# The last blocks of a hybrid decoder trunk: a kept order on VectorE and ACT, the products with the final weights on GpSimd, a last half block in two pieces

## The chip, the cores and the metric

The kernel runs on one core of one Trainium2 chip. The time is device microseconds for one execution, and the median of the runs is taken. "The profiled execution" is one further run, recorded by the hardware profiler. TensorE is called PE in the profile, VectorE DVE, ScalarE ACT, GpSimd POOL and SyncE SP.

## What is computed

A decoder trunk of two layers on 512 tokens of width 1024. Layer 0 is a convolution module and a feed-forward part, layer 1 is windowed attention and a feed-forward part. All that the change touches is the end: the down projection of the last feed-forward part, its residual, and the final RMSNorm.

```python
def rmsnorm(x, g):
    return x * lax.rsqrt(jnp.mean(x * x, axis=-1, keepdims=True) + EPS) * g
...
def swiglu_ffn(x, w_up, w_down):
    gate, up = jnp.split(x @ w_up, 2, axis=-1)
    return (jax.nn.silu(gate) * up) @ w_down
...
        h = h + swiglu_ffn(rmsnorm(h, norm_ffn[l]), ffn_w_up[l], ffn_w_down[l])
    return rmsnorm(h, norm_final)
```

## The kernel before

**Numbers.** A matrix product runs as three passes: weights and activations are both split into a high and a low part (`split`, `split_weights`, L277 and L280), and high x high, high x low and low x high are added up in one PSUM bank. A bank holds 128 partitions x 512 columns of float32. There are eight.

**Most of the span** is this stream of products: weights come in chunks of 128x1024 by DMA (SP issues them, L244), ACT and VectorE split them ahead of use, TensorE multiplies. In layer 1 the feed-forward part runs over pairs of hidden tiles; for most pairs a seven-product scheme for 2x2 blocks is used, and its down projection (`low_pairs`, matmuls at L862) adds into the rows of h directly: VectorE at L871, GpSimd at L869.

**The end** (L1521 to L1549) is what the change rewrites. Here the tokens lie on the partitions, so that the sum over the 1024 channels is a sum along a row. The last pair of hidden tiles (`hid`, its high and low part) is multiplied with the last two rows of `w_down` chunks (`whole`, one for each half g of the 1024 columns). The loop runs over NBLK = 4 blocks b of 128 tokens, and in it over the two halves g of 512 columns:

- six matmuls (L1531) into one bank: 2 tiles of hidden rows x 3 passes, 512 columns each;
- VectorE, L1533: `v = bank * rs + h`, the finished rows of h for this block and half, into `room[:, g]` in SBUF;
- ACT, L1535: the square of v with the sum of the row into a column of `ss` (the page shows it as an ACTIVATE and an ACTIVATION_READ_ACCUMULATOR);
- VectorE, L1537 for g = 0 and L1539 for g = 1: two small instructions on 128x1 that make the mean of squares plus EPS from the two sums;
- GpSimd, L1541, once a block: that number to the power -0.5 (called `last`, in the profile `rs<-ss,mhalf`);
- VectorE, L1542: the product of v with the final norm's weights, `gain`, into `room[:, 2 + g]`;
- after both halves, the scaling by `last`: VectorE for g = 1 (L1546), ACT for g = 0 (L1548);
- two stores of 128x512 to the output (L1549), g = 1 by SP's queue and g = 0 by ACT's.

Each engine works through its own queue in order. The order within a queue is set when the program is built: a list scheduler takes the instructions by a model of time. `tc.issue_after(x)` holds an instruction behind x in the program's order; before the change, nothing of the kind is used in this end. What came out for VectorE is, from the first L1533 on (b.g of each): L1533 0.0, L871, L1542 0.0, L1537 of block 0, L871, L1533 1.0, L1542 1.0, L1533 0.1, L1542 0.1, L1533 1.1, L1539 of block 0, L1533 2.0, L1537 of block 1, L1542 1.1, L1546 of block 0, L1542 2.0, L1539 of block 1, L1533 2.1, L1537 of block 2, L1533 3.0, L1546 of block 1, L1542 2.1, L1533 3.1, L1542 3.0, L1539 of block 2, L1537 of block 3, L1542 3.1, L1539 of block 3, L1546 of blocks 2 and 3. TensorE finishes the banks in the order 0.0, 1.0, 0.1, 1.1, 2.0, 2.1, 3.0, 3.1. GpSimd has nothing in this end but the four powers.

Of the kernel before, what the change touches and what calls it, by code (L numbers as in the profile page):

```python
# [11 lines left out]
F32 = mybir.dt.float32  # L12
F32R = mybir.dt.float32r
AF = mybir.ActivationFunctionType
ALU = mybir.AluOpType
# [3 lines left out]
P = 128  # L19
D = 1024  # L20
# [8 lines left out]
NBLK = S // P  # L29
BAND = 2 * P  # L30
NBUCKET = 32
EPS = 1e-6
# [160 lines left out]
def hybrid_trunk(ctx: ExitStack, tc: tile.TileContext, xT, W, prm_in, wdw_in, sinks, relb, onehot, fin, lead, out):  # L193
    nc = tc.nc
# [4 lines left out]
    small = ctx.enter_context(tc.tile_pool(name="small", bufs=4))  # L199
# [5 lines left out]
    def uid(s):  # L205
        ctr[0] += 1
        return f"{s}{ctr[0]}"

    def bank():
        return ps.tile([P, 512], F32, tag="bank", name=uid("bank"))  # L210
# [4 lines left out]
    def temp():  # L215
        return tmp.tile([P, 512], F32, tag="tmp", name=uid("tmp"))
# [65 lines left out]
    def advance():  # L282
        u = stream["use"]
        share[1] += share[0]
        while share[1] >= 1:
            share[1] -= 1
            next(preparing[0], None)
        load(u + DMA_AHEAD)
        while stream["split"] < min(len(PLAN), u + SPLIT_AHEAD):
            i = stream["split"]  # L290
            stream["split"] += 1
            if i in NATIVE:
                splits[i] = (raws.pop(i), None)
                continue
            hi = wpool.tile([P, 1024], F32R, tag="whi", name=uid("whi"))
            lo = wpool.tile([P, 1024], F32R, tag="wlo", name=uid("wlo"))
            splits[i] = (hi, lo)
            split_weights(hi, lo, raws.pop(i))
# [21 lines left out]
    def pace():  # L320
        g = seen[0] = seen[0] + 1
        for j in list(jobs):
            while j[2] < due_at(j[1], g):
                j[2] += 1
                if next(j[0], "end") == "end":
                    jobs.remove(j)
                    break

    def tick(n):
        while n > 0 and background:  # L330
            if next(background[0], "end") == "end":
                background.pop(0)
            else:
                n -= 1
# [10 lines left out]
    def get(*key):  # L345
        advance()
        pace()
        due[0] += rate[0]
        tick(int(due[0]))
        due[0] -= int(due[0])  # L350
        i = stream["use"]
        assert PLAN[i] == key, (PLAN[i], key)
        stream["use"] += 1
        hi, lo = splits.pop(i)
        n = {"kv": 4, "up": 4, "q": 4}.get(key[0], 2)
        sh = dict(a=n)
        return tuple(w and w.rearrange("p (a b) -> p a b", **sh) for w in (hi, lo))
# [95 lines left out]
    mhalf = cpool.tile([P, 4], F32, tag="mhalf", name="mhalf")  # L453
# [295 lines left out]
    def new_gates(pool):  # L749
        return pool.tile([P, 2, 2, 2, 256], F32, tag="up", name=uid("up"), bufs=3)  # L750

    def plain_pair(pair, rows, pool):

        banks = accs(512)
        steps = None
        for half in range(2):
            for which in range(2):
                w = get("up", 1, pair, half, which)
                order = [(k, m) for k in range(4) for m in range(2)]
                if half == 1:  # L760
                    order = [(k, m) for m in range(2) for k in range(4)]
                for k, m in order:
                    mm3(banks[which * 2 + m], [a[:, k, m * P:(m + 1) * P] for a in w], rows.x[half * 4 + k],
                        half == 0 and k == 0, half == 1 and k == 3)
                if half == 0 and which == 0:
                    rows.rms.step1()
                    continue

                if pair == 0:
                    steps = steps or rows.sums()  # L770
                    for _ in range(1 + half):
                        next(steps, None)
        rs_bc = rows.rms.step2().rearrange("p (s q) -> p s q", s=2)
        c = new_gates(pool)
        for m in range(2):
            t = temp()
            nc.vector.tensor_mul(t.rearrange("p (s q) -> p s q", s=2), banks[m].rearrange("p (s q) -> p s q", s=2), rs_bc)
            nc.scalar.activation(t, t, AF.Silu)
            nc.vector.tensor_mul(c[:, m, :, 0, :], banks[2 + m].rearrange("p (s q) -> p s q", s=2),
                                 t.rearrange("p (s q) -> p s q", s=2))  # L780
        return c
# [62 lines left out]
    def rows_of(g, t):  # L844
        return hT[:, g * 4:(g + 1) * 4, t * P:(t + 1) * P]
# [427 lines left out]
    for pair in range(lo0, hi0):  # L1273
        c = seven_pair("up0", pair, rows0, z0.tile([P, 2, 2, 2, 256], F32, tag="z0", name=uid("up"), bufs=5))
# [8 lines left out]
    if True:  # L1283
# [6 lines left out]
        x, rms = nxt.x, nxt.rms  # L1290
# [8 lines left out]
        for half in range(2):  # L1299
            whi, wlo = get("kv", 0, half)  # L1300
# [7 lines left out]
        for half in range(2):  # L1308
            whi, wlo = get("kv", 1, half)
            for k in range(4):  # L1310
                xh, xl = xkv[half * 4 + k]
# [4 lines left out]
            if half == 0:  # L1316
                rs_bc = rms.step2()
                rs = rms.rs
# [4 lines left out]
        for n in range(4):  # L1323
            nc.vector.tensor_scalar(vq[:, n].rearrange("p a g c -> p (a g c)"), vb[n][:, 0:256], rs[:, n:n + 1], None,
                                    op0=ALU.mult)
# [126 lines left out]
        for part in range(2):  # L1452
            for g in range(2):
# [3 lines left out]
                if part == 0:  # L1457
# [3 lines left out]
                    for m0, kp in ((0, 0), (0, 1), (2, 0), (2, 1)) if g else ((0, 0), (2, 0), (0, 1), (2, 1)):  # L1461
                        order = [(k, m) for k in range(2) for m in (m0, m0 + 1)]
                        if kp:
                            order = [(k, m) for m in (m0, m0 + 1) for k in range(2)]
# [12 lines left out]
                for m in range(4):  # L1477
                    i = g * 4 + m
# [20 lines left out]
    for kind, pair in STEPS1:  # L1499
# [6 lines left out]
        if by_seven(1, pair):  # L1506
            c = seven_pair("up", pair, nxt, new_gates(pool7), flip if pair == SEVENS[0] else None)
        else:
            c = plain_pair(pair, nxt, pool7)
# [8 lines left out]
        gain = quads.tile([P, 2, D], F32, tag="quad", name=uid("gain"))[:, 0]  # L1518
        nc.sync.dma_start(gain, fin.to_broadcast([P, D]))

    whole = [get("down", 1, LAST, g) for g in range(2)]  # L1521
    for b in range(NBLK):
        tok, rs = slice(b * P, (b + 1) * P), nxt.rms.rs[:, b:b + 1]
        room = quads.tile([P, 4, 512], F32, tag="quad", name=uid("room"))
        ss = small.tile([P, 4], F32, tag="ss", name=uid("ss"))
        for g, (whi, wlo) in enumerate(whole):
            acc = bank()
            for k in range(2):
                xh, xl = (hid[:, e, k, tok] for e in range(2))
                for n, (x, w) in enumerate(((xh, whi), (xh, wlo), (xl, whi))):  # L1530
                    nc.tensor.matmul(acc, x, w[:, k, :], start=k == 0 and n == 0, stop=k == 1 and n == 2)  # L1531
            v, o = room[:, g], room[:, 2 + g]
            nc.vector.scalar_tensor_tensor(v.rearrange("p (i c) -> p i c", i=4), acc.rearrange("p (i c) -> p i c", i=4), rs,  # L1533
                                           rows_of(g, b), op0=ALU.mult, op1=ALU.add)
            nc.scalar.activation(temp(), v, AF.Square, accum_out=ss[:, g:g + 1])  # L1535
            if g == 0:
                nc.vector.tensor_scalar(ss[:, 2:3], ss[:, 0:1], 1.0 / D, EPS, op0=ALU.mult, op1=ALU.add)  # L1537
            else:
                nc.vector.scalar_tensor_tensor(ss[:, 3:4], ss[:, 1:2], 1.0 / D, ss[:, 2:3], op0=ALU.mult, op1=ALU.add)  # L1539
                last = small.tile([P, 1], F32, tag="rs1", name=uid("rs1"))  # L1540
                nc.gpsimd.tensor_tensor(last, ss[:, 3:4], mhalf[:, 0:1], op=ALU.pow)  # L1541
            nc.vector.tensor_mul(o, v, gain[:, g * 512:(g + 1) * 512])  # L1542
        for g in range(2):
            o = room[:, 2 + g]
            if g:
                nc.vector.tensor_scalar(o, o, last[:, 0:1], None, op0=ALU.mult)  # L1546
            else:
                nc.scalar.mul(o, o, last[:, 0:1])  # L1548
            (nc.sync if g else nc.scalar).dma_start(out[tok, g * 512:(g + 1) * 512], o)  # L1549
    seven.close()  # L1550


# [25 lines left out]
```

## Time and profile before

| what | value |
|---|---|
| median of 3 runs | 1048.46 us (1048.23 to 1049.19) |
| the profiled execution, own time | 1049.17 us |
| its span, first to last instruction | 1047.3 us |
| mean granted TensorE clock | 0.997 |
| busy over the span: PE, DVE, ACT, POOL | 1034.8, 777.3, 615.4, 465.9 us |
| first L1533 of the end starts | 1027.10 us |
| last matmul starts | 1037.77 us |
| last scaling on ACT starts (two merged) | 1041.72 us |

Times inside a profile count from its first instruction. A row of the timeline reads: start, duration, engine, line, operation, output<-inputs, form, count; in square brackets stands how long the engine was idle before it and what ended that. Instructions of one engine overlap a little: the next one starts some 0.1 us before the record of the one ahead ends. The profiled execution's own time lies 1.9 us above its span and 0.7 us above the median.

### The profile page before, as it was taken

The page shows a single profiled execution, that of the slowest core. Times are in us where ns is not written, and L with a number is a line of the kernel's source. Part 1 is how long each engine was busy: PE and PEld are TensorE (multiplying, and loading weights), DVE is VectorE, ACT ScalarE, POOL GpSimd, SP SyncE. Part 2 cuts the span into 40 slices and gives each one's busy share as a digit, 9 for nine tenths or more (in the row PEclk, how much of TensorE's full clock was granted, in tenths as well). Part 3 has the DMA queues.
Part 4 walks back from the last instruction along what each step waited for, and adds up shares of the span by engine and source line. Part 5 has one row for each costly group of instructions (what it writes and reads, how often), then busy time and mean ns, then how long its engine had stood idle before and what let it go on. Part 6 is the DMA issues. An engine that isn't in the chain of part 4 may idle for free.

```text
span 1047.3 us, 17725 instructions
## 1 busy us (share of the span) xinstructions
PE 1034.8 (99%) x6598; PEld 934.7 (89%) x6598; DVE 777.3 (74%) x1207; ACT 615.4 (59%) x1062; POOL 465.9 (44%) x559
## 2 busy tenths in 40 slices
PE   8999999999999999999999999999999999999996
PEld 7888889999988899999888877788989999898995
DVE  3999988978779766775536556678686877868677
ACT  3887897845576555554334555466655556554653
POOL 3999999930335312223214255506442343423131
PEclk9999999999999999999999999999999999999998
DMA  9998847998899979979978776863789898786542
GB/s 350 349 341 116 259 131 218 259 233 268 221 250 275 284 220 243 306 236 289 297 212 240 205 192 184 208 207 128 238 251 309 273 251 274 202 253 195 195 140 81
DMA packets 67011, 245.72 MB, mean 235 GB/s; under 512 B 7499, under 2 KB 13804, under 8 KB 66156
## 3 DMA queue, kind: packets, MB, share of 16 engines
q1 hardware_dynamic: 54108, 199.44, 55.4%
q0 software_dynamic: 12096, 44.05, 23.4%
q8 instruction: 52, 0.85, 0.3%
q10 hardware_dynamic: 720, 1.10, 0.3%
q14 instruction: 35, 0.29, 0.1%
HBM read 239.31 MB, written 93.32 MB: 318 GB/s over the span
## 4 chain that ended last, share of the span: by engine, by line
PE 96%; POOL 1%; DVE 1%; issue 1%; DMA 1%; ACT 0%; SPq 0%; POOLq 0%
PE bank L363 19%; PE bank L365 19%; PE bank L364 19%; PE bank L920 10%; PE bank L862 9%; PE bank L395 5%; PE bank L396 3%; PE bank L361 3%; PE bank L1373 1%; PE bank L1415 1%; PE bank L1402 1%; PE bank L1018 1%; DMA both<-in_lead_dram 1%; POOL pr L962 1%; PE bank L908 1%
## 5 line engine op out<-in xcount | busy, mean ns | idle before, releaser
L280 DVE TENSOR_TENSOR wlo<-raw,whi 128x1024 fp32r<-128x1024 f32 x249 | 326.1, 1317 | 136.0 <-ACT whi L277 134.4
L277 ACT CAST whi<-raw 128x1024 fp32r<-128x1024 f32 x249 | 260.6, 1050 | 273.4 <-PE bank L364 189.4
L363 PE MATMUL bank<-quad,whi 128*128 128x256 f32 (+1 forms) x928 | 292.3, 317 | 0.0
L365 PE MATMUL bank<-quad,wlo 128*128 128x256 f32 (+1 forms) x928 | 291.6, 315 | 0.0
L364 PE MATMUL bank<-quad,whi 128*128 128x256 f32 (+1 forms) x928 | 291.6, 315 | 0.0
L363 PEld LDWEIGHTS bank<-quad,whi 128*128 128x128 f32 x928 | 176.6, 191 | 12.2 <-issue 1.6
L365 PEld LDWEIGHTS bank<-quad,wlo 128*128 128x128 f32 x928 | 176.6, 190 | 11.4 <-issue 0.6
L364 PEld LDWEIGHTS bank<-quad,whi 128*128 128x128 f32 x928 | 176.7, 191 | 11.0 <-issue 0.2
L822 POOL TENSOR_TENSOR up<-up 128x512 f32<-128x512 f32 x32 | 56.6, 1770 | 282.1 <-ACT up L819 282.1
L962 POOL TENSOR_TENSOR pr<-pr,pr 128x256 f32<-128x256 f32 x208 | 157.7, 805 | 2.2 <-ACT pr L961 2.2
L363 PE MATMUL bank<-rows,whi 128*128 128x256 f32 x512 | 144.6, 283 | 0.0
L364 PE MATMUL bank<-rows,whi 128*128 128x256 f32 x512 | 144.6, 283 | 0.0
L365 PE MATMUL bank<-rows,wlo 128*128 128x256 f32 x512 | 144.4, 282 | 0.0
L969 DVE SCALAR_TENSOR_TENSOR bank<-apad,wdw,bank 128x256 f32<-128x256 f32 x248 | 112.5, 485 | 3.4
L961 ACT ACTIVATE pr<-apad,wdw 128x256 f32<-128x256 f32 x208 | 98.7, 503 | 15.1 <-POOL pr L962 13.2
L920 PE MATMUL bank<-quad,w 128*128 128x256 f32 x448 | 98.7, 380 | 0.0
L364 PEld LDWEIGHTS bank<-rows,whi 128*128 128x128 f32 x512 | 97.7, 191 | 0.3
L363 PEld LDWEIGHTS bank<-rows,whi 128*128 128x128 f32 x512 | 97.7, 191 | 0.3
L365 PEld LDWEIGHTS bank<-rows,wlo 128*128 128x128 f32 x512 | 97.6, 191 | 0.0
L920 PEld LDWEIGHTS bank<-quad,w 128*128 128x128 f32 x448 | 84.9, 190 | 11.8 <-DVE bank L969 0.2
L395 PE MATMUL bank<-quad,whi 128*128 128x512 f32 x212 | 75.9, 398 | 0.0
L474 POOL TENSOR_TENSOR tmp<-tmp,tmp 128x256 f32<-128x256 f32 (+1 forms) x28 | 26.8, 957 | 104.6 <-ACT tmp L470 99.7
(225 smaller groups left out, 1671.4 us busy)
## 6 DMA issues: line engine op xcount, KB each, us to landing
raw<-in_W_dram SPq DMA_DIRECT2D x177, 512.0 KB, 5.6
raw<-sum SPq DMA_DIRECT2D x84, 512.0 KB, 4.7
sum<-in_W_dram SPq DMA_DIRECT2D x48, 512.0 KB, 5.9
sum<-in_W_dram POOLq DMA_DIRECT2D x42, 512.0 KB, 9.0
sum<-sum POOLq DMA_DIRECT2D x42, 512.0 KB, 9.6
sum<-in_W_dram SPq DMA_DIRECT2D x4, 3072.0 KB, 26.1
w<-in_W_dram SPq DMA_DIRECT2D x14, 512.0 KB, 9.0
sum<-in_W_dram SPq DMA_DIRECT2D x4, 1536.0 KB, 33.7
```

Of the source, the lines that this page charges most:

```text
L277: on_act = nc.scalar.copy(hi, src).ins
L280: latest[:] = [on_act, lo_engine[0].tensor_sub(lo, src, f32(hi)).ins]
L363: nc.tensor.matmul(out, w[0], x[0], start=start, stop=False, **kw)
L364: nc.tensor.matmul(out, w[0], x[1], start=False, stop=False, **kw)
L365: nc.tensor.matmul(out, w[1], x[0], start=False, stop=stop, **kw)
L395: nc.tensor.matmul(first[2], first[0], first[1], start=start, stop=False)
L822: pool_op(nc.gpsimd.tensor_mul(gate, gate, c[:, m, :, 1, :]))
L862: nc.tensor.matmul(out, x, w[:, ws], start=first and e == 0 and i == 0, stop=e == 1 and i == 2, skip_group_check=True)
L920: mm = nc.tensor.matmul(self.pb[:, w * W2:(w + 1) * W2], w1_of(ct, w, k), x[k] if x else xg[k][:, tok], start=k == 0, stop=k == KT - 1)
L961: on_act = nc.scalar.mul(pr, a[:, j:j + W2], tap(j))
L962: on_pool = pool_op(nc.gpsimd.tensor_add(pr, acc, pr))
L969: on_dve = nc.vector.scalar_tensor_tensor(yt if i == nd - 1 else c, src, tap(i), c if i else self.shift, op0=ALU.mult, op1=ALU.add)
```

## The change

- `then(eng, op)` issues an operation behind the one that the same engine was given last through `then`. The L1533 kind, the squares, the second sums, the scalings and the last product go through it, so that VectorE and ACT work in the order in which the program names them.
- The products with `gain` go to GpSimd, except for the last one (block 3, g = 1), which stays on VectorE.
- The scalings of a block are named one block later, behind the evacuations of the next one (`before`).
- The last half block is cut in two pieces of 256 columns, each with six matmuls, an evacuation, a square and a sum.
- All stores go to SP's queue, except for the last block's g = 0, which stays on ACT's.

```diff
+    order = {"vector": None, "scalar": None}
+    def then(eng, op):
+        with tc.issue_after(order[eng]) if order[eng] else nullcontext():
+            order[eng] = op().ins
+    def scale(b, room, last, g):
+        o = room[:, 2 + g]
+        if g:
+            then("vector", lambda: nc.vector.tensor_scalar(o, o, last[:, 0:1], None, op0=ALU.mult))
+        else:
+            then("scalar", lambda: nc.scalar.mul(o, o, last[:, 0:1]))
+        (nc.sync if g or b < NBLK - 1 else nc.scalar).dma_start(out[b * P:(b + 1) * P, g * 512:(g + 1) * 512], o)
+    before = None
     for b in range(NBLK):
...
-        for g, (whi, wlo) in enumerate(whole):
-            acc = bank()
+        ends = b == NBLK - 1
+        pieces = ((0, 0, 4), (1, 0, 2), (1, 2, 4)) if ends else ((0, 0, 4), (1, 0, 4))
+        for n, (g, i0, i1) in enumerate(pieces):
+            cols = slice(i0 * P, i1 * P)
+            acc = bank()[:, 0:(i1 - i0) * P]
+            whi, wlo = whole[g]
...
-            nc.vector.scalar_tensor_tensor(v..., acc..., rs, rows_of(g, b), op0=ALU.mult, op1=ALU.add)
-            nc.scalar.activation(temp(), v, AF.Square, accum_out=ss[:, g:g + 1])
+            then("vector", lambda: nc.vector.scalar_tensor_tensor(
+                v..., acc..., rs, rows_of(g, b)[:, i0:i1], op0=ALU.mult, op1=ALU.add))
+            then("scalar", lambda: nc.scalar.activation(temp()[:, cols], v, AF.Square, accum_out=ss[:, n:n + 1]))
+            if not (ends and g):
+                nc.gpsimd.tensor_mul(room[:, 2 + g], room[:, g], gain[:, g * 512:(g + 1) * 512])
+            if before and n == len(pieces) - 1:
+                for g in range(2):
+                    scale(*before, g)
+            if n == 0:
+                nc.vector.tensor_scalar(ss[:, 4:5], ss[:, 0:1], 1.0 / D, EPS, op0=ALU.mult, op1=ALU.add)
             else:
-                nc.vector.scalar_tensor_tensor(ss[:, 3:4], ss[:, 1:2], 1.0 / D, ss[:, 2:3], op0=ALU.mult, op1=ALU.add)
...
-            nc.vector.tensor_mul(o, v, gain[:, g * 512:(g + 1) * 512])
-        for g in range(2):
...
+                then("vector", lambda: nc.vector.scalar_tensor_tensor(
+                    ss[:, 4 + n:5 + n], ss[:, n:n + 1], 1.0 / D, ss[:, 3 + n:4 + n], op0=ALU.mult, op1=ALU.add))
+        last = small.tile([P, 1], F32, tag="rs1", name=uid("rs1"))
+        nc.gpsimd.tensor_tensor(last, ss[:, 3 + len(pieces):4 + len(pieces)], mhalf[:, 0:1], op=ALU.pow)
+        if ends:
+            then("vector", lambda: nc.vector.tensor_mul(room[:, 3], room[:, 1], gain[:, 512:1024]))
+        before = b, room, last
+    for g in range(2):
+        scale(*before, g)
```

Built, the two programs differ from the first evacuation of the end on, and nowhere ahead of it. VectorE's order is now (b.g): evacuation 0.0, L871, first sum of block 0, L871, evacuation 0.1, second sum of block 0, evacuations 1.0 and 1.1, scaling of block 0, both sums of block 1, evacuations 2.0 and 2.1, first sum of block 2, scaling of block 1, second sum of block 2, evacuation 3.0, first piece of 3.1, first and second sum of block 3, second piece of 3.1, scaling of block 2, third sum of block 3, the last product, scaling of block 3. ACT's order: squares 0.0, 0.1, 1.0, 1.1, scaling of block 0, squares 2.0, 2.1, scaling of block 1, squares 3.0 and the two pieces of 3.1, scaling of blocks 2 and 3. GpSimd's: for each of the blocks 0 to 2 two products, then the power; for block 3 one product, then the power. TensorE's order of banks stays.

More of the change, by code (lines that the diff above doesn't have):

```diff
@@ L1524, in hybrid_trunk @@
         room = quads.tile([P, 4, 512], F32, tag="quad", name=uid("room"))
-        ss = small.tile([P, 4], F32, tag="ss", name=uid("ss"))
-        for g, (whi, wlo) in enumerate(whole):
-            acc = bank()
+        ss = small.tile([P, 8], F32, tag="ss", name=uid("ss"))
+        ends = b == NBLK - 1
[4 more added lines that the diff above has]
+            whi, wlo = whole[g]
@@ L1528, in hybrid_trunk @@
             for k in range(2):
                 xh, xl = (hid[:, e, k, tok] for e in range(2))
[L1530 to L1534, printed above, removed]
@@ L1535, in hybrid_trunk @@
-            nc.scalar.activation(temp(), v, AF.Square, accum_out=ss[:, g:g + 1])
-            if g == 0:
-                nc.vector.tensor_scalar(ss[:, 2:3], ss[:, 0:1], 1.0 / D, EPS, op0=ALU.mult, op1=ALU.add)
-            else:
-                nc.vector.scalar_tensor_tensor(ss[:, 3:4], ss[:, 1:2], 1.0 / D, ss[:, 2:3], op0=ALU.mult, op1=ALU.add)
-                last = small.tile([P, 1], F32, tag="rs1", name=uid("rs1"))
-                nc.gpsimd.tensor_tensor(last, ss[:, 3:4], mhalf[:, 0:1], op=ALU.pow)
@@ L1542, in hybrid_trunk @@
-            nc.vector.tensor_mul(o, v, gain[:, g * 512:(g + 1) * 512])
-        for g in range(2):
[L1544 to L1549, printed above, removed]
+                for m, (x, w) in enumerate(((xh, whi), (xh, wlo), (xl, whi))):
+                    nc.tensor.matmul(acc, x, w[:, k, cols], start=k == 0 and m == 0, stop=k == 1 and m == 2)
@@ new lines, in hybrid_trunk @@
+            v = room[:, g, cols]
+            then("vector", lambda: nc.vector.scalar_tensor_tensor(
+                v.rearrange("p (i c) -> p i c", c=P), acc.rearrange("p (i c) -> p i c", c=P),
+                rs, rows_of(g, b)[:, i0:i1], op0=ALU.mult, op1=ALU.add))
+            then("scalar", lambda: nc.scalar.activation(temp()[:, cols], v, AF.Square, accum_out=ss[:, n:n + 1]))
+            if not (ends and g):
+                nc.gpsimd.tensor_mul(room[:, 2 + g], room[:, g], gain[:, g * 512:(g + 1) * 512])
```

## The prediction

> **What bounds the kernel now.** First the page: the chain that ended last, by engine.
>
> ```profile
> PE 96%; POOL 1%; DVE 1%; issue 1%; DMA 1%; ACT 0%; SPq 0%; POOLq 0%
> ```
>
> TensorE carries 96% of the span, and nothing ahead of the end is touched. So only the last 20 us count; the windows show who is busy there.
>
> ```profile
> core 0: us, PE busy (x) PEld busy (x) DVE busy (x) ACT busy (x) POOL busy (x), PEclk, DMA share, GB/s
> 1032.00:1037.00 5.00, 5.00 (x24) 4.14 (x23) 4.66 (x11) 3.34 (x9) 0.60 (x2) 1.00 0.04 14
> 1037.00:1042.00 5.00, 1.16 (x6) 0.62 (x4) 4.61 (x12) 2.95 (x8) 1.86 (x3) 1.00 0.52 196
> 1042.00:1047.30 5.30, 0.00 (x0) 0.00 (x0) 0.70 (x2) 1.06 (x2) 0.25 (x1) 0.50 0.54 198
> ```
>
> TensorE is done soon after 1038; from 1032 to 1042 VectorE is busy 9.3 of 10 us, GpSimd 2.5. The chain of waits, in order of time, says the same:
>
> ```profile
> 1028.64 3.64 PE bank L1531 x16
> 1032.28 0.02 issue
> 1032.31 0.76 DVE room L1533
> ...
> 1040.60 0.07 DVE ss L1537
> 1040.68 0.01 issue
> 1040.68 1.01 POOL rs L1541
> 1041.70 0.03 issue
> 1041.72 1.33 ACT room L1548 x2
> ```
>
> From 1032.31 to 1040.68 the end hangs on VectorE (the rows left out are its own, but for a short issue), then on GpSimd's power and ACT's last scaling, which ends at 1043.05. What follows, the last store and the close, takes 4.25 us to the span's end and stays: ACT still stores the last block's g = 0, SP its g = 1. So I compare when ACT's last scaling ends, and add the difference to the median. (The profiled execution took 1049.17, 0.7 over the median; a profile of the changed kernel should stand the same way.)
>
> **What the change removes.** Durations of the groups in this end:
>
> ```profile
> L1533 DVE SCALAR_TENSOR_TENSOR room<-bank,rs,h 128x512 f32<-128x512 f32 x8 | 5.9, 747 | 1.0 <-PE bank L1531 1.0
> L1542 DVE TENSOR_TENSOR room<-room,gain 128x512 f32<-128x512 f32 x8 | 5.5, 686 | 0.1
> L1535 ACT ACTIVATE tmp<-room 128x512 f32<-128x512 f32 x8 | 5.0, 625 | 8.0 <-DVE room L1533 7.9
> L1548 ACT ACTIVATE room<-room,rs 128x512 f32<-128x512 f32 x4 | 2.8, 720 | 2.1 <-POOL rs L1541 2.1
> L1541 POOL TENSOR_TENSOR rs<-ss,mhalf 128x1 f32<-128x1 f32 x4 | 2.7, 682 | 17.2 <-DVE ss L1539 14.0 <-DVE ss L1537 3.1
> L1546 DVE TENSOR_SCALAR room<-room,rs 128x512 f32<-128x512 f32 x4 | 1.9, 483 | 0.5 <-POOL rs L1541 0.4
> L1539 DVE SCALAR_TENSOR_TENSOR ss<-ss 128x1 f32<-128x1 f32 x4 | 0.6, 154 | 0.0
> ```
>
> Seven of eight products leave VectorE: 7 x 0.60 (0.686 less some 0.09 of overlap) = 4.2 us, nearly all from the chain above. If nothing else became late, TensorE would set the end; that is the first rival.
>
> **What it adds on GpSimd.** Seven 128x512 products of two SBUF operands, and the powers stand behind them in GpSimd's queue. The nearest rows are the same operation and size:
>
> ```profile
> L869 POOL TENSOR_TENSOR h<-h,tmp x10: 1282/1296/1841, 781.8 to 1021.1; 128x512 f32<-128x512 f32 x10
> L822 POOL TENSOR_TENSOR up<-up x32: 1292/1828/2310, 384.2 to 1017.9; 128x512 f32<-128x512 f32 x32
> ```
>
> Undisturbed it takes 1.29 us (1.25 from start to start: two of L869 in 2.54), twice VectorE's 0.686. The longer ones start beside a long VectorE subtraction (below). I take 1.29, bounds 1.28 and 1.83.
>
> When can GpSimd start? The first product (block 0, g = 0) is early. The second needs evacuation 0.1, and that needs its bank:
>
> ```profile
> 1030.33 0.75 DVE L1533 SCALAR_TENSOR_TENSOR room<-bank,rs,h 128x512 f32<-128x512 f32 x1 [0.52 <-PE bank L1531]
> 1032.31 0.75 DVE L1533 SCALAR_TENSOR_TENSOR room<-bank,rs,h 128x512 f32<-128x512 f32 x1 [0.49 <-PE bank L1531]
> ```
>
> The row at 1032.31 is evacuation 0.1; it ends at 1033.06, and GpSimd reacts some 0.08 later: 1033.14. From there six products and four powers stand in one queue: 6 x 1.25 + 4 x 0.53 = 9.6, so the last power ends at 1042.75 at best. Before, the last two powers were these:
>
> ```profile
> 1040.68 1.56 POOL L1541 TENSOR_TENSOR rs<-ss,mhalf 128x1 f32<-128x1 f32 x2 [3.14 <-DVE ss L1537]
> ...
> 1040.58 0.69 DVE L1542 TENSOR_TENSOR room<-room,gain 128x512 f32<-128x512 f32 x1
> ```
>
> They ended at 1042.24. The queue alone is already 0.5 us later than the chain it replaces.
>
> **What the kept order adds.** ACT squares that half, and reads out the sum:
>
> ```profile
> 1033.09 0.64 ACT L1535 ACTIVATE tmp<-room 128x512 f32<-128x512 f32 x1 [4.49 <-DVE room L1533]
> 1033.63 0.19 ACT L1535 ACTIVATION_READ_ACCUMULATOR tmp<-room 128x1 f32 x1
> ```
>
> The row at 1030.33 is evacuation 1.0, done before 0.1 while VectorE had nothing else. Now it stands behind block 0's second sum, which waits for ACT's square of 0.1 (1033.09 to 1033.82). So VectorE idles from about 1029.5 to 1032.3, and evacuation 1.0 slips from 1030.33 to 1033.9 or later. Behind each such sum, and behind each scaling that waits for a power, all later evacuations are queued, and for these wait ACT's squares and GpSimd's products.
>
> **Do the two engines hold each other?** The rows say yes:
>
> ```profile
> 1020.68 0.75 DVE L871 SCALAR_TENSOR_TENSOR h<-bank,rs,h 128x512 f32<-128x512 f32 x1 [1.96 <-PE bank L862]
> 1021.35 2.12 DVE L280 TENSOR_TENSOR wlo<-raw,whi 128x1024 fp32r<-128x1024 f32 x1
> ...
> 1025.97 1.21 DVE L280 TENSOR_TENSOR wlo<-raw,whi 128x1024 fp32r<-128x1024 f32 x1
> ...
> 1019.84 2.54 POOL L869 TENSOR_TENSOR h<-h,tmp 128x512 f32<-128x512 f32 x2
> ...
> L882 DVE TENSOR_SCALAR quad<-both,prm x8: 349/354/883, 3.9 to 10.4; 128x256 f32<-128x256 f32 x8
> ...
> 7.90 4.85 POOL L474 TENSOR_TENSOR tmp<-tmp,tmp 128x256 f32<-128x256 f32 x6 [2.23 <-ACT tmp L470]
> ...
> L520 DVE SCALAR_TENSOR_TENSOR quad<-h,prm,quad x40: 477/748/1789, 147.7 to 706.1; 128x512 fp32r<-128x512 f32 x24, 128x256 fp32r<-128x256 f32 x16
> ```
>
> The subtraction with two SBUF operands that starts at 1021.35 takes 2.12 instead of 1.21 (1025.97), and ends 1.09 after GpSimd's additions end at 1022.38: it waited for them. L882 is a scaling from SBUF to SBUF, like L1546: 0.35 us, but up to 0.88 among L474's additions. L520, the operation of the sums, with two SBUF operands, goes from 0.75 to 1.79. The other way round, the first power at 1040.68 took 1.01 (in the chain) beside VectorE's last product, the other, in the same row, the 0.55 that is left. An evacuation, with one operand in PSUM, isn't held: L871 at 1020.68 takes its usual 0.75 while GpSimd adds.
>
> So three kinds of instruction now meet GpSimd's products: the scalings of 128x512 (held, as L882), the second and third sums of 128x1 with two SBUF operands, and the last product against the last power (held, as at 1040.68). Whether an instruction of 128x1 is held, no row settles: the one L1539 near a power ran in 0.16, but right behind VectorE's own product. Bounds for each sum: nothing (0.15), or the rest of a product, up to 1.29. I take held, since its operation is held at every larger size (L520).
>
> The Trainium skill, "SBUF — State Buffer", section "Who interferes with whom", bears on it: VectorE with two SBUF inputs or in a two-port mode and GpSimd exclude each other for a whole instruction, and it names no size below which this ends. By it the sums are held; a reading without it leaves the third case below.
>
> **The sum.** Once GpSimd works without a gap, a round of one block is a ring: evacuation 0.75, reaction 0.08, product g = 0 1.29, scaling of the block before, held behind it, 0.40, product g = 1, held behind the scaling, 1.29, second sum, held behind that product, 0.07: 3.88 us, against TensorE's 2.7 a block (16 matmuls in 3.64 us, in the chain, make 12 in 2.73).
> - Sum of block 0 is held till the second product ends (1033.14 + 1.29 = 1034.43); evacuation 1.0 starts at 1034.5.
> - Two rounds: evacuation 3.0 starts at 1034.5 + 7.7 = 1042.2.
> - Evacuation 0.75 + 0.08 + product 1.29: 1044.3; the sum of the first piece is held till then, + 0.07.
> - Second piece of 256 columns: evacuation 0.48 (L969, below), square and read-out some 0.53 (an estimate: 512 columns take 0.73 above, bounds half of that and all of it), third sum 0.15, to 1045.5.
> - The last power, held by the last product as at 1040.68: 1.05 and 0.08, to 1046.7. ACT's last scaling 0.72: 1047.45.
>
> That is 4.4 after 1043.05. The same arithmetic, with scalings and products held, puts the old end 0.1 late; I take **4.3: 1048.46 + 4.3 = 1052.8 us**.
>
> **Edits at nothing.** The rows for these and for the pieces:
>
> ```profile
> 1037.77 0.39 PE L1531 MATMUL bank<-whi,hid 128*128 128x512 f32 x1
> ...
> L969 DVE SCALAR_TENSOR_TENSOR bank<-apad,wdw,bank 128x256 f32<-128x256 f32 x248 | 112.5, 485 | 3.4
> ...
> 1042.47 0.95 ACTq L1549 DMA_DIRECT2D out_dram<-room  x2
> ```
>
> The two pieces: twelve matmuls instead of six, at most 0.1 us on TensorE, hidden since it is done near 1038 and VectorE comes for the last piece at 1044.4; they gain nothing either, for the same reason. Uncovered they would cost that 0.1. SP's seven stores: SP has nothing else queued, an issue is at most 0.48 (two in 0.95), and the last three are over 0.5 apart; in a pile they would cost up to 0.48 each.
>
> **Rivals.**
> 1. *Faster: TensorE sets the end.* Last matmul 1038.25 (started 1037.77 before, 0.39 long, and 0.1), evacuation 0.5, square 0.53, sum 0.15, power 0.6, ACT 0.72: 1040.8, that is 1046.2 us. It needs GpSimd to keep up: its queue is ahead of the old end only if a product costs under 1.16 us (1033.14 + 6p + 2.1 = 1042.24). The rows start at 1.28. Chance 0.04.
> 2. *GpSimd's queue alone,* no holding: 1042.75 + 0.72 = 1043.5: 1048.9. Against it L882 and 1021.35. 0.10.
> 3. *Scalings and the last product are held, the 128x1 sums are not.* Two products held by a scaling (0.46 each), the last power by its late sum (0.64, behind a held scaling) and by the last product (0.49): 1042.75 + 2.05 + 0.75 = 1045.55: 1050.9 us. 0.31.
> 4. *Products at 1.83:* five of them on the path, 5 x 0.54 = 2.7 on top of mine: 1055.5. Against it: no long VectorE instruction is left here. 0.05.
>
> **The numbers.** My own case has 0.50; the third rival's and mine together 0.81, so the range spans them: 1050.2 (0.7 below 1050.9, if a hold is lost) to 1053.6 (0.8 above mine, half a product). About 0.2%, 2.1 us, is what a measurement of this kernel can tell from no change. Slower by more: 0.50 + 0.23 (three quarters of the third rival, whose 1050.9 lies just above 1050.56) + 0.05 = 0.78; within: 0.08 + 0.10 = 0.18; faster 0.04.
>
> **What would show it.** Right: evacuation 1.0 at 1034.5, scalings on VectorE of 0.9 to 1.3 us instead of 0.48, sums of 0.7 to 1.5 instead of 0.15, GpSimd busy without gaps from 1033, evacuation 3.0 near 1042.2, the last power near 1046.7. Sums of 0.15 with long scalings: the third rival. Scalings of 0.48: the second. Wrong altogether: products under 1.2 us, or the last evacuation waiting for TensorE.

## The result, and the profile after

The changed kernel takes 1051.8 us (median of 15 runs), the kernel before 1049.03 on the same chips (15 runs): ratio 1.0025, 95% interval 1.0017 to 1.0033, slower by 1.8 to 3.5 us. The profiled execution has a span of 1049.6 us against 1047.3.

First the page's chain by engine, then the windows of the end (columns as before).

```profile
PE 88%; ACT 3%; DVE 3%; issue 2%; POOL 2%; DMA 1%; POOLq 0%; SPq 0%; DVEq 0%; ACTq 0%
```

```profile
core 0: us, PE busy (x) PEld busy (x) DVE busy (x) ACT busy (x) POOL busy (x), PEclk, DMA share, GB/s
1032.00:1037.00 5.00, 5.00 (x26) 4.25 (x25) 4.10 (x7) 2.78 (x7) 3.95 (x4) 1.00 0.00 0
1037.00:1042.00 5.00, 0.90 (x8) 0.70 (x6) 4.81 (x8) 2.13 (x6) 4.59 (x6) 0.98 0.52 194
1042.00:1047.00 5.00, 0.00 (x0) 0.00 (x0) 2.52 (x8) 2.83 (x8) 2.05 (x2) 0.50 0.37 136
```

The fall from 96% to 88% is not the loss: the end is under 2% of the span. Most of it lies between 100 and 200 us, in the convolution stage, where the chain goes through other links of the same program (L962, L961 and L969 beside TensorE). The windows are the reading: GpSimd goes from 2.5 to 8.5 us busy between 1032 and 1042, and VectorE is nearly as busy as before (8.9 us against 9.3) with six products fewer in this stretch. It is busy with being held, as the rows below show. The chain of waits through the end:

```profile
1028.31 3.64 PE bank L1550 x16
1031.95 0.03 issue
1031.98 0.76 DVE room L1552
1032.74 0.02 issue
1032.76 0.73 ACT tmp L1555 x2
...
1034.04 1.40 DVE room L1552 x2
1035.44 1.07 DVE room L1531
...
1036.68 1.00 DVE ss L1564
1037.67 0.67 DVE room L1552
...
1039.89 1.21 DVE ss L1564
1041.11 0.67 DVE room L1552
1041.78 0.07 issue
1041.85 1.27 POOL room L1557
...
1045.42 0.72 ACT room L1533
```

Two instructions of 128x1 (L1564) stand in it with 1.00 and 1.21 us. The groups of the end, to be laid beside those of before:

```profile
L1557 POOL TENSOR_TENSOR room<-room,gain 128x512 f32<-128x512 f32 x7 | 9.3, 1335 | 9.8 <-DVE room L1552 9.5
L1552 DVE SCALAR_TENSOR_TENSOR room<-bank,rs,h 128x512 f32<-128x512 f32 x7 | 5.0, 738 | 2.9 <-PE bank L1550 2.9
L1564 DVE SCALAR_TENSOR_TENSOR ss<-ss 128x1 f32<-128x1 f32 x5 | 3.1, 626 | 1.4 <-ACT tmp L1555 1.3
L1531 DVE TENSOR_SCALAR room<-room,rs 128x512 f32<-128x512 f32 x4 | 2.8, 705 | 0.4 <-POOL rs L1567 0.4
L1567 POOL TENSOR_TENSOR rs<-ss,mhalf 128x1 f32<-128x1 f32 x4 | 2.6, 655 | 1.6 <-DVE ss L1564 1.3
```

The evacuations are as long as before (0.74). The second sums (with the third one of the last block) went from 154 to 626 ns in the mean, the scalings from 483 to 705. Timeline of VectorE, then of GpSimd:

```profile
1026.77 0.73 DVE L1552 SCALAR_TENSOR_TENSOR room<-bank,rs,h 128x512 f32<-128x512 f32 x1
...
1031.98 0.75 DVE L1552 SCALAR_TENSOR_TENSOR room<-bank,rs,h 128x512 f32<-128x512 f32 x1 [2.87 <-PE bank L1550]
1033.52 0.60 DVE L1564 SCALAR_TENSOR_TENSOR ss<-ss 128x1 f32<-128x1 f32 x1 [0.79 <-ACT tmp L1555]
1034.04 1.40 DVE L1552 SCALAR_TENSOR_TENSOR room<-bank,rs,h 128x512 f32<-128x512 f32 x2
1035.36 1.14 DVE L1531 TENSOR_SCALAR room<-room,rs 128x512 f32<-128x512 f32 x1
...
1036.68 1.00 DVE L1564 SCALAR_TENSOR_TENSOR ss<-ss 128x1 f32<-128x1 f32 x1
...
1039.26 0.71 DVE L1531 TENSOR_SCALAR room<-room,rs 128x512 f32<-128x512 f32 x1
1039.89 1.21 DVE L1564 SCALAR_TENSOR_TENSOR ss<-ss 128x1 f32<-128x1 f32 x1
1041.03 1.13 DVE L1552 SCALAR_TENSOR_TENSOR room<-bank,rs,h 128x512 f32<-128x512 f32 x2
...
1043.02 0.16 DVE L1564 SCALAR_TENSOR_TENSOR ss<-ss 128x1 f32<-128x1 f32 x1 [0.24 <-ACT tmp L1555]
```

```profile
1032.81 1.30 POOL L1557 TENSOR_TENSOR room<-room,gain 128x512 f32<-128x512 f32 x1 [3.93 <-DVE room L1552]
1034.20 0.58 POOL L1567 TENSOR_TENSOR rs<-ss,mhalf 128x1 f32<-128x1 f32 x1
1034.92 2.73 POOL L1557 TENSOR_TENSOR room<-room,gain 128x512 f32<-128x512 f32 x2
...
1038.42 2.67 POOL L1557 TENSOR_TENSOR room<-room,gain 128x512 f32<-128x512 f32 x2
1041.18 0.55 POOL L1567 TENSOR_TENSOR rs<-ss,mhalf 128x1 f32<-128x1 f32 x1
1041.85 1.27 POOL L1557 TENSOR_TENSOR room<-room,gain 128x512 f32<-128x512 f32 x1
1044.44 0.94 POOL L1567 TENSOR_TENSOR rs<-ss,mhalf 128x1 f32<-128x1 f32 x1 [1.33 <-DVE ss L1564]
```

Lay them over each other: the sum at 1033.52 ends at 1034.12, where GpSimd's product ends (1034.11); the sum at 1036.68 ends at 1037.68, where the pair of products ends (1037.65); the sum at 1039.89 ends at 1041.10, where the next pair ends (1041.09).

The programs are equal up to the first evacuation, so I count from its start (the profiles of this study reach it between 1026.18 and 1027.59 us, which is scatter). "End part" is from there to the end of the last scaling.

| us after the first evacuation's start | before | after |
|---|---|---|
| evacuation 1.0 starts | 3.23 | 7.27 |
| evacuation 3.0 starts | 10.44 | 14.26 |
| last power ends | 15.15 | 18.61 |
| last scaling on ACT ends: the end part | 15.95 | 19.37 |
| from there to the span's end | 4.25 | 3.46 |

So the spans differ by 3.42 in the end part, less 0.79 in the close, less 0.33 of scatter: 2.3 us.

### The profile page after: what moved, and what is told of

It reads as the page before. It is cut to its first block, busy times and chain, and to the rows that moved or that the text cites. A ratio compares the mean times of both kernels' runs of the same rounds, so it can differ in the third digit from the quotient of the medians.

```text
span 1049.6 us, 17752 instructions
## 1 busy us (share of the span) xinstructions
PE 1035.1 (99%) x6604; PEld 935.2 (89%) x6604; DVE 776.5 (74%) x1202; ACT 614.9 (59%) x1064; POOL 474.0 (45%) x566
## 4 chain that ended last, share of the span: by engine, by line
PE 88%; ACT 3%; DVE 3%; issue 2%; POOL 2%; DMA 1%; POOLq 0%; SPq 0%; DVEq 0%; ACTq 0%
PE bank L363 19%; PE bank L365 19%; PE bank L364 19%; PE bank L862 9%; PE bank L920 7%; PE bank L395 5%; PE bank L396 3%; PE bank L1373 1%; PE bank L1415 1%; PE bank L1402 1%; ACT pr L961 1%; DVE bank L969 1%; POOL pr L962 1%; DMA sum<-sum 1%; PE bank L908 1%
## 5 line engine op out<-in xcount | busy, mean ns | idle before, releaser
L962 POOL TENSOR_TENSOR pr<-pr,pr 128x256 f32<-128x256 f32 x208 | 157.5, 799 | 2.2 <-ACT pr L961 2.0
L969 DVE SCALAR_TENSOR_TENSOR bank<-apad,wdw,bank 128x256 f32<-128x256 f32 x248 | 112.4, 484 | 3.4
L961 ACT ACTIVATE pr<-apad,wdw 128x256 f32<-128x256 f32 x208 | 98.4, 502 | 15.0 <-POOL pr L962 12.9
```

Of the source, the lines that this page charges most:

```text
L961: on_act = nc.scalar.mul(pr, a[:, j:j + W2], tap(j))
L962: on_pool = pool_op(nc.gpsimd.tensor_add(pr, acc, pr))
L969: on_dve = nc.vector.scalar_tensor_tensor(yt if i == nd - 1 else c, src, tap(i), c if i else self.shift, op0=ALU.mult, op1=ALU.add)
```

## The experiments

**Theory A**: the change keeps a wrong order (evacuation 1.0 behind block 0's second sum), and mutual holding of VectorE and GpSimd turns it into a ring. **Theory B**: GpSimd's products and the holding are the whole cost. The runs come in two groups of four, each beside its own runs of the kernel before (medians 1049.26 and 1048.91); end parts are from one profile each. They can stand for the time: in the changed kernel and in all eight runs, what end part and close (the stretch from there to the span's end) differ from before comes within 0.5 us of what the medians differ.

**1. The kept order with all products on VectorE.**

```diff
-                nc.gpsimd.tensor_mul(room[:, 2 + g], room[:, g], gain[:, g * 512:(g + 1) * 512])
+                then("vector", lambda: nc.vector.tensor_mul(room[:, 2 + g], room[:, g], gain[:, g * 512:(g + 1) * 512]))
```

> The changed kernel, but with all products with the final weights on VectorE, each behind its evacuation in the kept order; GpSimd has only the four powers. End part = from the start of the first evacuation to the end of the last scaling on ACT: 15.95 us before, 19.37 changed. Theory A (the kept order puts evacuation 1.0 behind block 0's sum, and the mutual holding of the two engines comes on top): the order alone already costs, end part 18.5, time some 1 us under the changed kernel and some 2 us over before; no scaling or sum on VectorE is longer than 0.5. Theory B (GpSimd's products and the holding are the whole cost): end part 16 to 16.5, time within 0.5 us of before.

1051.07 us, ratio 1.0019 (1.0010 to 1.0027); end part 18.93, where Theory A had 18.5. Nothing on VectorE is held:

```profile
L1531 DVE TENSOR_SCALAR room<-room,rs 128x512 f32<-128x512 f32 x4 | 1.9, 481 | 0.4 <-POOL rs L1567 0.4
...
L1564 DVE SCALAR_TENSOR_TENSOR ss<-ss 128x1 f32<-128x1 f32 x5 | 0.8, 158 | 0.9 <-ACT tmp L1555 0.8
```

With the products on VectorE, what is left of the change loses 3.0 us of end part, against the 3.4 of the whole. That is not the order alone, since the two pieces are still there. Run 5 prices the pieces at 0.9 us, though beside products on GpSimd, so some 2.1 us is the order's: an estimate, for no run has this order without pieces and with the products on VectorE. Theory B, with 16 to 16.5, is out either way.

**2. The products on GpSimd, the scheduler's order.**

```diff
-            nc.vector.tensor_mul(o, v, gain[:, g * 512:(g + 1) * 512])
+            (nc.vector if g and b == NBLK - 1 else nc.gpsimd).tensor_mul(o, v, gain[:, g * 512:(g + 1) * 512])
```

> The kernel before, with seven of eight products on GpSimd and nothing else changed; the scheduler orders VectorE anew (evacuations 0.0, 1.0, 0.1, 1.1, then the sum of block 0). Theory A: GpSimd gets work from 1030 on and is not the bound; holdings occur (one scaling near 1.4, a sum near 1.1) but have slack, end part 16.4, time within 0.6 us of before. Theory B: the products and the holding cost whatever the order, end part 18.5 to 19.4, time 2.5 us over before.

1049.98 us, 1.0012 (1.0004 to 1.0021); end part 16.99. GpSimd starts its second product at 4.1 after the first evacuation, not 6.0, and the end part loses 1.04 us, against the change's 3.42. That is Theory A's side, but it had 16.4 and under 0.6 us (the medians differ by 0.7; one of the eleven runs took 1053.96): two scalings, of 1.41 and 1.57, were held, where one near 1.4 was expected. So the products on GpSimd and their holds are not free in this order.

**3. The sums in a form with one tensor operand.**

```diff
-                then("vector", lambda: nc.vector.scalar_tensor_tensor(
+                then("vector", lambda: nc.vector.tensor_scalar(
                     ss[:, 4 + n:5 + n], ss[:, n:n + 1], 1.0 / D, ss[:, 3 + n:4 + n], op0=ALU.mult, op1=ALU.add))
```

> The changed kernel with the second and third sums in another form: one tensor operand and a scalar per partition instead of two tensor operands. If a small sum is held because it has two operands in SBUF: all sums 0.15, the scalings on VectorE still held (1.2 to 1.5), end part 17.6 to 17.9, time 1.5 us under the changed kernel. If it is held for its being behind GpSimd whatever its form: sums 0.6 to 1.2 as in the changed kernel, end part 19.4, no difference.

1050.1 us, 1.0009 (1.0000 to 1.0018); end part 17.86.

```profile
L1531 DVE TENSOR_SCALAR room<-room,rs 128x512 f32<-128x512 f32 x4 | 3.5, 886 | 0.4 <-POOL rs L1567 0.4
...
L1564 DVE TENSOR_SCALAR ss<-ss 128x1 f32<-128x1 f32 x5 | 1.1, 211 | 1.3 <-ACT tmp L1555 1.0
```

The same sums at the same places, three of them in the middle of a product, take 0.20 to 0.21 us each instead of 0.63 in the mean: they were held for their two operands in SBUF, at a size of 128x1 too. (The operation changes along with the operands, but it is not what counts: the evacuations are the old operation with one operand in a bank, and take 0.74 beside the same products.) The scalings, still held, got longer (0.89 in the mean), since VectorE now comes to them, the second above all, earlier in GpSimd's product; the end part got 1.5 us shorter all the same. The rule that the prediction took from the Trainium skill ("SBUF — State Buffer", "Who interferes with whom"), which names no size, holds here down to one element a partition.

**4. As 3, and all scalings on ACT.**

```diff
-        if g:
-            then("vector", lambda: nc.vector.tensor_scalar(o, o, last[:, 0:1], None, op0=ALU.mult))
-        else:
-            then("scalar", lambda: nc.scalar.mul(o, o, last[:, 0:1]))
+        then("scalar", lambda: nc.scalar.mul(o, o, last[:, 0:1]))
```

> As the run with one-operand sums, and all scalings on ACT: on VectorE nothing but the last product can meet GpSimd. Theory A (and the queue of GpSimd as the bound once no one is held): six products and four powers in a row from the second evacuation's end, 9.6 to 10.1 us, the last power ends some 16.1 after the first evacuation's start, end part (last of two scalings on ACT) 17.5; time some 1.9 us under the changed kernel, 1 us over before. If the holding had cost nothing, end part 19.4 or more, since ACT has more to do.

1049.39 us, 1.0002 (0.9994 to 1.0011); end part 17.65, the last power at 16.28. GpSimd's rows:

```profile
1034.92 2.54 POOL L1554 TENSOR_TENSOR room<-room,gain 128x512 f32<-128x512 f32 x2
1037.43 0.55 POOL L1564 TENSOR_TENSOR rs<-ss,mhalf 128x1 f32<-128x1 f32 x1
1037.95 2.49 POOL L1554 TENSOR_TENSOR room<-room,gain 128x512 f32<-128x512 f32 x2
...
1042.44 0.93 POOL L1564 TENSOR_TENSOR rs<-ss,mhalf 128x1 f32<-128x1 f32 x1 [0.26 <-DVE ss L1561]
```

With no one to hold it, a pair of products is down from 2.73 to 2.54, and GpSimd works without a gap from its second product to the end of its seventh (1042.18): up to there its queue is the bound, as the second rival had it. The last power then waits 0.26 for the third sum and is held by the last product (0.93). The time came out better than the end part says, because the last four stores, one ACT scaling apart, leave less behind (3.1 us from the last scaling to the span's end).

**5. The last half block whole again.**

```diff
-        pieces = ((0, 0, 4), (1, 0, 2), (1, 2, 4)) if ends else ((0, 0, 4), (1, 0, 4))
+        pieces = ((0, 0, 4), (1, 0, 4))
```

> The changed kernel with the last half block whole again: six matmuls, one evacuation, one square, one sum. If the pieces gain nothing because TensorE is long done when VectorE comes (theory A): the end part is not longer than the changed kernel's 19.4, rather 18.6, since one evacuation, one square and a third sum drop out of the chain; time 0 to 0.8 us under the changed kernel. If the pieces shorten the last chain as they would behind a TensorE that sets the end: end part 19.8, time 0.4 us over the changed kernel.

1050.76 us, 1.0019 (1.0009 to 1.0028); end part 18.47. The pieces cost 0.9 us of end part: a square, a read-out and a sum more in the last chain, and nothing gained, since TensorE had ended 5 us before the second piece was fetched. (The time moves the same way, but the intervals of the two ratios overlap.)

**6. Stores of g = 0 on ACT's queue in all blocks.**

```diff
-        (nc.sync if g or b < NBLK - 1 else nc.scalar).dma_start(
+        (nc.sync if g else nc.scalar).dma_start(
```

> The changed kernel with the stores of g = 0 on ACT's queue in all blocks, as before. If the queue of the stores is nothing: end part 19.4, and the stretch from the last scaling to the span's end 3.5, both within 0.2; time within 0.4 us of the changed kernel. If SP's queue had cost or gained: the stretch goes back to the 4.3 of before.

1051.3 us, 1.0024 (1.0015 to 1.0034); end part 19.27, then 3.45. No difference from the changed kernel, though the scheduler also put the first sum of block 2 behind the scaling of block 1 here. The run shows besides how well an end part repeats: to 0.1 us.

**7. The same work in another kept order.** The end is written as a list of words, issued one by one through `then`, on GpSimd too: v evacuation (its matmuls ahead of it), q square, m product, s sum (a: the first), r power, z scaling, then block, half, piece (a, b), and last the engine (v VectorE, a ACT, p GpSimd).

```diff
+    SEQ = ("v00v q00a m00p s0av v10v q10a m10p v01v s1av q01a m01p v11v s0v q11a v20v m11p q20a v21v r0p s1v "
+           "m20p z00a z01v q21a r1p v30v m21p z10a s2av s2v q30a v31av r2p z11v q31aa m30p s3av v31bv s3bv q31ba "
+           "z20a s3v z21v r3p m31v z30a z31v")
```

> The changed kernel's work, pieces and stores, products on GpSimd and two-operand sums included, in another kept order on the three engines: evacuation 1.0 ahead of 0.1, each block's second sum and its scaling behind the evacuations of the block after. Theory A (a wrong order kept, which the holding turns into a ring): evacuation 1.0 at 3.2 after the first, GpSimd busy from 4.1 on, the last scaling ends 16.3 to 17 after the first evacuation's start, time within 0.8 us of before, 2 to 3 us under the changed kernel, though there are holds of 0.3 to 1.3 as before. If the holding is the cost whatever the order: end part over 18.5.

1048.76 us, 1.0001 (0.9992 to 1.0010); end part 16.1. The instructions are the changed kernel's, the holds too: sums of 451 ns, scalings of 740.

```profile
L1576 DVE TENSOR_SCALAR room<-room,rs 128x512 f32<-128x512 f32 x4 | 3.0, 740 | 0.1
...
L1567 DVE SCALAR_TENSOR_TENSOR ss<-ss 128x1 f32<-128x1 f32 x5 | 2.3, 451 | 0.2
```

Only the order differs, and the 2.6 us are gone. One thing came with it that the list doesn't say: TensorE, too, finishes the bank of 1.0 earlier (evacuation 1.0 at 2.27, not 3.2).

```profile
1029.84 0.75 DVE L1552 SCALAR_TENSOR_TENSOR room<-bank,rs,h 128x512 f32<-128x512 f32 x1
...
1032.75 0.75 DVE L1552 SCALAR_TENSOR_TENSOR room<-bank,rs,h 128x512 f32<-128x512 f32 x1 [1.50 <-PE bank L1551]
```

No run separates that from the rest, but the rows say that it carries little: VectorE stands idle for 1.50 us before the next evacuation (0.1), and GpSimd, not busy from 4.1 on as expected, stands idle from 4.5 to 6.0 after the first. An evacuation 1.0 that came one microsecond later would have found room there.

**8. A version made from the runs.** Order as in 7, sums as in 3, the half block whole as in 5, and for g = 1 product and scaling in one VectorE instruction behind the power (word f; `!` marks the one-operand sum).

```diff
+    SEQ = ("v00v q00a m00p s0av v10v q10a m10p s1av v01v q01a v11v s0!v v20v q11a r0p q20a s1!v m20v r1p z00a "
+           "v21v f01v q21a s2av z10a s2!v v30v r2p f11v q30a m30p v31v z20a s3av f21v q31a s3!v r3p z30a f31v")
...
+                then(eng, lambda: nc.vector.scalar_tensor_tensor(o, room[:, g], lasts[b], part, op0=ALU.mult, op1=ALU.mult))
```

> A version made from what the runs say: kept order as in the run ahead, the sums in the one-operand form, and for g = 1 product and scaling in one VectorE instruction (v x last x gain) after the power, so that VectorE loses one instruction a block; g = 0 products on GpSimd for blocks 0, 1 and 3, on VectorE for 2; the last half block whole. Theory A: GpSimd has one product a block and is no bound, VectorE 2.2 us a block against TensorE's 2.7, so TensorE sets the pace: last scaling 14.7 to 15.3 after the first evacuation's start against 15.95 before, time 0.7 to 1.7 us under before. If the fused instruction and GpSimd's products hold each other more than that: 16 or more.

1047.42 us, ratio to before 0.9986 (0.9977 to 0.9994): faster than both kernels, by 0.6 to 2.4 us against before. End part 14.98. Its windows:

```profile
1032.00:1037.00 5.00, 5.00 (x24) 4.14 (x23) 3.79 (x8) 2.79 (x7) 1.55 (x3) 1.00 0.01 3
1037.00:1042.00 5.00, 1.61 (x8) 0.99 (x6) 4.21 (x10) 3.57 (x9) 2.81 (x3) 0.87 0.73 270
```

```profile
1038.77 1.71 POOL L1557 TENSOR_TENSOR room<-room,gain 128x512 f32<-128x512 f32 x1
```

VectorE has slack between 1032 and 1037 (3.79 of 5 us), and the last evacuation starts at 11.68, 0.65 us behind TensorE's end (11.03), with a fused instruction between. That TensorE sets the pace is shown only up to 6.3 us after the first evacuation. From there the chain of waits goes through VectorE, ACT and the product in the last row, which took 1.71 us beside two fused instructions: some mutual holding is left. The run changes several things at once; what each of them brings isn't shown.

## Why the prediction was right, and where it was off

**The products on GpSimd and when they start.** Right: 1.27 to 1.30 us undisturbed; the second one starts 6.04 after the first evacuation, as worked out. The queue alone is right too: in run 4 the seventh product ends 15.10 after the first evacuation, and a power of 0.55 right behind it would end at 15.65, the forecast 0.5 later than the 15.15 of before. (The power itself ended at 16.28, since it waited and was held.)

**The kept order.** Right in the place and its time: evacuation 1.0 at 7.27 after the first, 7.4 forecast. Underrated in its weight: I counted it as one part, behind the holding. Run 1 shows that it loses 3.0 us of end part together with the pieces and without any product on GpSimd, run 7 that in a better order the same kinds of hold cost nothing that the time shows. The two don't add up: with the products on VectorE the late start is paid there, with the products on GpSimd it is paid in the ring.

**The holding.** Right for all three kinds, if not always in the size that I had named as a sign: scalings of 1.14 and 0.71 (0.9 to 1.3 named), sums of 0.60, 1.00 and 1.21 (0.7 to 1.5 named), the last power 0.94 where 1.05 was taken. GpSimd worked with hardly a gap from its second product on, but only up to 1043.1; then it waited 1.33 us for the third sum. The small sums, the open point on which I chose, are held (run 3), so the third rival falls. The time alone would not have said so: as a difference to the kernel before, the third rival's 2.4 us lies nearer to the measured 2.6 than my 4.3. One hold of the ring failed: the sum of the first piece took 0.16; GpSimd's product was just ending, and it had waited for ACT's read-out instead. It cost nothing either way.

**The sum.** That 1051.8 lies only 1.0 below 1052.8 is luck in part: the kernel before took 1049.03 in these runs, 0.6 more than the median to which I had added. As a difference, 4.3 was forecast and 2.6 measured (by the ratio; 2.8 by the medians). Two terms were mis-sized, both to the same side.
- A round of the ring: 3.88 forecast, 3.56 and 3.43 measured. I had counted the scaling between two products at its full 0.40, so 2.98 for the pair; the pairs took 2.73 and 2.67. Against run 4's pairs without a scaling (2.54 and 2.49) only some 0.19 is added to GpSimd's time. That the scaling does part of its work while it waits would explain it, but no run shows that. The rest is the next evacuation, which starts 0.07 to 0.08 before the sum's record ends, where I had added 0.07 behind the product. The two rounds make 0.7 of the 0.98 below.
- The close, which I had said stays: 4.25 went to 3.46. I had compared only who issues the last store. A row of the DMA engines for 8 us from 1040 on, in cells of 0.2 us (each digit is the busy share in tenths), first before, then after:

```profile
DMA  9970000000000006999999999999930000000000
```

```profile
DMA  0000899999910000000000008996699702899999
```

Before, four stores of 256 KB come within 0.9 us and keep the engines full for 2.8 us, 0.7 us each. After, the two stores ahead are through at 1046.4, before the last two start at 1046.7: two are in the line, not four. Run 4, with the four spread over 2.0 us, has 3.1. When the first of the line is issued counts as well: run 8 has two in the line too, but both issued as the last scaling ends, where the changed kernel's first was issued 0.2 us ahead of that, and its stretch is 3.85.

Together: 20.35 forecast for the end part against 19.37, 0.98 too long, less the 0.1 that I had taken off, and 0.79 of the close: 1.7 us, the distance between the 4.3 forecast and the 2.6 measured.

**The pieces.** I had put both their gain and their cost at nothing. That was half right: nothing gained, but 0.9 us of end part lost (run 5). The prediction had the second read-out and the third sum in its chain, but I never laid them against a last half block in one piece; TensorE's matmuls were all that I had priced for the cut. The stores on SP's queue, put at nothing too, did cost nothing (run 6).

**The first rival** (TensorE sets the end) was rightly small: in the changed kernel TensorE ends at 11.13 and the last piece is fetched at 16.32. Run 8 comes nearer to it, with less than half of the products on GpSimd.

## What to carry to other kernels

Before you move work to an idle engine, see whether the two engines hold each other: lay the two timelines over each other and look for instructions of the one that end where instructions of the other end. Here VectorE got rid of six products in ten microseconds and stayed nearly as busy. In an order kept by hand, one instruction that waits holds up all behind it: put nothing ahead of work that is ready but what is ready as early. In run 7, with sums and scalings one block behind, the same work took no longer than before. Find out which engine ends last before you cut its last piece: here it was not TensorE, and the cut cost 0.9 us of end part.

## What the runs showed of the hardware

- A VectorE instruction on 128x1 with two operands in SBUF waits for GpSimd's running product: up to 1.21 us instead of 0.15 (the changed kernel). With one tensor operand and a scalar per partition from SBUF the same sum takes 0.21 and doesn't wait (run 3).
- A held scaling of 128x512 (0.48 alone) adds only 0.19 to GpSimd's pair of products (2.73 with it, 2.54 without, in run 4).
- Four stores of 256 KB issued within 0.9 us, two by SP's queue and two by ACT's, kept the DMA engines busy for 2.8 us, 0.7 us each. With the stores of g = 0 moved from SP's queue to ACT's, the stretch from the last scaling to the end stays the same (run 6: 3.45 against 3.46).
